# A block of dilated attention and gated delta rule: ScalarE's functions grouped by table, z's columns behind the keys', the decays' sums beside the values, levels of the inverse by a counted wait

## The chip, the core and the metric

The kernel runs on one core of a Trainium2 chip. The core has TensorE (matmuls, in the profile PE, its weight loads PEld), VectorE (DVE), ScalarE (ACT), GpSimd (POOL) and SyncE (SP), which issues nearly all DMAs here. Each engine works through its own queue in order, and engines wait for each other by semaphores. The metric is device time in microseconds, the median of some runs. The profile is of one execution; its TensorE clock is given as the share of full speed that was granted.

## What is computed

One transformer block over 1024 tokens of width 1024, in float32: modulation by a vector c, an RMS norm, one projection of 3600 columns, attention over dilated windows (8 heads of 64), a gated delta rule (8 heads of 64), an output projection, and a gated feed-forward part. The change lies in the delta rule:

```python
def _gated_deltanet(q, k, v, z, b_logit, a_logit, conv_w, a_log, dt_bias, norm_g):
    qkv = silu(_causal_conv(concatenate([q, k, v], -1), conv_w))     # four taps
    q, k, v = split(qkv, 3, -1)                                      # 8 heads of 64
    q = _l2norm(q) * HEAD_DIM ** -0.5
    k = _l2norm(k)
    beta = sigmoid(b_logit)
    g = -exp(a_log) * softplus(a_logit + dt_bias)
    o = _chunk_gated_delta_rule(q, k, v, g, beta)
    return _rmsnorm(o, norm_g) * silu(z)
```

Within a chunk the sums of g over the tokens (gcum) give decays exp(gcum_i - gcum_j); the keys' products with each other, times decay and beta, are a strictly lower triangular matrix A; I + A is inverted against the values and keys; then the state goes from chunk to chunk:

```python
    v_new = u_i - w_i @ state
    o_i = (q_i * exp(g_i)) @ state + qk_i @ v_new
    state = state * exp(g_last) + (k_i * exp(g_last - g_i)).T @ v_new
```

The modulation is `silu(c) @ w_ada + b_ada`, six vectors of 1024; the later ones are needed only after attention.

## The kernel before

**Tiling.** Activations are kept transposed, 128 of the 1024 features to a partition tile and 1024 tokens along the free axis. A product at float32's precision is three matmuls: weights and activations are split into a rounded part (hh, wh) and a rest (hl, wl), with the pairs hh-wh, hl-wh, hh-wl. `wsplit` (L209) loads a slab of weights through SyncE, ScalarE rounds it (L215), GpSimd takes the rest (L216); there are 3 raw and 5 split buffers. The kernel works on chunks of 128 tokens, eight of them, for two groups g of four heads.

**Filler.** Projections that nothing waits for yet come from a generator, `others` (L1103), a unit at a time: a unit of `proj_d` (L571) is three matmuls of 512 columns and is counted as 0.64 us, one of `proj_t` (L579) three of 256 columns, counted as 0.32. These counts are nominal. Its order is z of group 0 (20.48 us nominal), then keys kd, queries qd and values vd of group 1 (20.48 each), z of group 1, the attention's values (40.96), and its keys and queries (81.92). `mixed` (L1123) adds one row of the modulation (`modulation`, L1081: a DMA of 256 KB, four small matmuls, L196) whenever 1.9 us of filler have gone by, unless `quiet` is set; there are 64 rows in 8 sums, all in one PSUM bank, and after each sum VectorE turns it (L203) and adds the bias (L207).

**Order.** A scheduler puts the instructions on the queues at build time: it takes, for each engine, what it reckons to be ready, in the program's order, unless something is marked urgent. `tc.issue_after(i)` only fixes issue order: what is traced inside comes behind i on i's engine. Where delta-rule work would come too early on TensorE, `turn(name)` (L552) looks up FILL (L41): so much filler is traced first, and the step is issued behind its last matmul. `hold` (L1136) does the same ahead of the levels of the inverse: it traces filler until a named projection is done (`until`, L1143) and then so many us more (LEVELS, L31: group 0 "qd" and 4, group 1 "z1" and 28). These are lower bounds: the scheduler can still put later filler in front.

**The front.** The projections of the first keys and queries (their second half L600 to L605) and of values end at about 113 us. `decays` (L645 to L668) makes, in three PSUM banks, the sums Gc of the decays within a chunk (L654, L655), their totals (L657, and ScalarE's Exp L658), edec and eG (L660, L661), and Gc transposed (L663), which goes to DRAM as G and comes back as rows for each head (`delta_rows`, L680), masked on GpSimd (L692).

**A group of the delta rule** (`delta`, L1163). Conv and Silu of keys and queries (`conv`, L529; Silu at L536); transposes and squares (`delta_turn`, L705); Ln (L1175 in group 0, L741 in group 1) and Exp (L743) of the keys' sums of squares, the root; 32 Exps of the decay tiles dt (L747); the products of keys with keys and queries (L776, the kk products) and VectorE's products with the decays (L782); stores of the diagonal 32x32 blocks (L789); Exp of the rows for the queries (L815); conv, Silu, transposes (L833) of the values (`delta_v`); then `delta_inverse` (L843): the blocks come back as nt, VectorE inverts all of them in 31 dependent double steps (L862, L866), stores them (L869) and reads them back as tn (L871). The levels put the 128x128 inverses together from them for four heads (L894 lv, L909, L913, L923 lw, L931 lx). `delta_scan` (L945) then goes through the chunks. Between the groups `delta_early` (L1152) does the conv, Silu and squares of group 1's keys and queries. z's columns go through Silu on ScalarE as each block leaves PSUM (`z_evac`, L611). After group 1 come attention with the rest of the filler, the output projection and the feed-forward part, which the change does not touch.

## Time and profile before

| what | us |
|---|---|
| median of 3 runs | 1498.29 (1481.16 to 1502.68) |
| the profiled execution | 1498.45 |
| its span | 1496.7 |
| TensorE busy | 1405.0 |
| VectorE, ScalarE, GpSimd busy | 873.6, 669.6, 302.2 |
| granted clock, mean | 0.961 |

The stages that matter, by their first and last instruction on TensorE: front to 113.5 us, group 0 up to the levels 113.5 to 241.1, its levels to 267.2, its scan, the early part of group 1 and group 1 up to its levels to 412.8, these levels to 449.5, group 1's scan to 491.7, then filler alone to 522.3, and attention. A busy TensorE at a granted clock of 0.5 does half the work; idle time of an engine that bounds nothing costs nothing. In a row of the profile the last bracket holds the idle time of the engine before the instruction and what ended it.

### The profile page before, as it was taken

Reading aid. Unit: us, or ns where it says so; the run is one execution under the profiler, and the core shown is the slowest. Engines: PE = TensorE matmul, PEld = TensorE weight load, DVE = VectorE, ACT = ScalarE, POOL = GpSimd, SP = SyncE. Lnnn points to the kernel's source line nnn. Section 1 sums busy time; section 2 is a strip of 40 time slices with the busy share of each in tenths; the row PEclk is TensorE's granted clock in tenths of the full one; section 3 lists DMA queues with packets and bytes.
Section 4 is the critical chain, followed back from the end, with each engine's and each line's share of the span. In section 5 each row is a group of like instructions: output and inputs, shape, how many; then the busy total and the mean of one; then the engine's idle time right before and its main releaser. Section 6 shows DMA issues by size and latency. Waiting matters only on the chain. (4 is left out here: it accounts for less than half of the span.)

```text
span 1496.7 us, 24578 instructions
## 1 busy us (share of the span) xinstructions
PE 1405.0 (94%) x8984; PEld 1140.2 (76%) x8984; DVE 873.6 (58%) x1664; ACT 669.6 (45%) x1283; POOL 302.2 (20%) x275
## 2 busy tenths in 40 slices
PE   7998989988999989999998899999999999999986
PEld 4677857867888768777876678888888888878765
DVE  3786843665736041466327986757575755454675
ACT  3487413357123353676337633333333333445453
POOL 2344412335104332444253000000000000000011
PEclk9998999999959999999999999999999999999998
DMA  8736563475502526633384374535363636656664
GB/s 307 249 94 170 142 205 122 146 241 142 165 20 78 167 84 166 186 106 109 104 263 141 108 245 136 197 121 199 116 205 106 216 107 202 226 191 191 192 206 164
DMA packets 171345, 244.64 MB, mean 163 GB/s; under 512 B 33014, under 2 KB 76327, under 8 KB 171224
## 3 DMA queue, kind: packets, MB, share of 16 engines
q1 hardware_dynamic: 171224, 243.07, 52.0%
q8 instruction: 71, 1.16, 0.4%
q14 instruction: 50, 0.41, 0.1%
HBM read 180.25 MB, written 67.48 MB: 166 GB/s over the span
## 5 line engine op out<-in xcount | busy, mean ns | idle before, releaser
L1747 POOL TENSOR_TENSOR y<-y,gfr 128x512 f32<-128x512 f32 x8 | 12.9, 1633 | 669.4 <-DMA xr<-x_d 639.6
L1502 DVE TENSOR_TENSOR wl_db<-wr_db,wh_db 128x512 fp32r<-128x512 f32 x77 | 54.2, 704 | 95.1 <-ACT wh_db L1501 95.1
L1501 ACT CAST wh_db<-wr_db 128x512 fp32r<-128x512 f32 x77 | 48.0, 623 | 112.7 <-PE X L1690 58.6
L1690 PE MATMUL X<-wl_db,wh_da 128*128 128x512 f32 x176 | 71.4, 406 | 9.1 <-DVE wl_db L1502 9.1
L1690 PE MATMUL X<-wh_db,wl_da 128*128 128x512 f32 x176 | 70.9, 403 | 0.0
L1690 PE MATMUL X<-wh_db,wh_da 128*128 128x512 f32 x176 | 68.3, 393 | 0.0
L1263 POOL TENSOR_SCALAR X<-X,sc 128x128 f32<-128x128 f32 (+7 forms) x64 | 48.0, 753 | 69.5 <-DVE sc L1262 55.9
L1261 ACT ACTIVATE X<-X,sc 128x128 f32<-128x128 f32 (+7 forms) x64 | 49.5, 775 | 22.3 <-DVE sc L1256 16.6
L1256 DVE CUSTOM_DVE_ANT_0 X<-S,ng 128x512 f32<-128x512 f32 (+3 forms) x64 | 36.9, 586 | 33.5 <-PE S L1253 22.5
L1502 DVE TENSOR_TENSOR wl_da<-wr_da,wh_da 128x512 fp32r<-128x512 f32 x77 | 53.9, 700 | 3.6 <-ACT wh_da L1501 3.6
L567 PE MATMUL wo<-yh,wh_wo 128*128 128x512 f32 x128 | 53.1, 416 | 2.4 <-ACT yh L1359 1.7
L1222 DVE SCALAR_TENSOR_TENSOR QS<-raw,QS 64x1024 fp32r<-64x1024 f32 x8 | 12.6, 1573 | 70.5 <-ACT QS L1221 70.5
L567 PE MATMUL wo<-yh,wl_wo 128*128 128x512 f32 x128 | 51.4, 403 | 0.0
L567 PE MATMUL wo<-yl,wh_wo 128*128 128x512 f32 x128 | 51.1, 401 | 0.0
L1501 ACT CAST wh_da<-wr_da 128x512 fp32r<-128x512 f32 x77 | 47.4, 615 | 7.5 <-PE wua L1512 5.8
L567 PE MATMUL g_a<-hh,wh_a 128*128 128x512 f32 x128 | 50.6, 395 | 0.0
L567 PE MATMUL g_a<-hh,wl_a 128*128 128x512 f32 x128 | 50.5, 395 | 0.0
L567 PE MATMUL g_a<-hl,wh_a 128*128 128x512 f32 x128 | 50.3, 393 | 0.0
L1293 PE MATMUL y<-et,va 128*64 128x128 f32 x576 | 47.7, 288 | 1.3 <-ACT et L1281 1.3
L1690 PEld LDWEIGHTS X<-wl_db,wh_da 128*128 128x128 f32 x176 | 34.4, 195 | 18.3 <-DVE wl_db L1502 11.0
L1501 ACT CAST wh_wg_s<-wg_s 128x512 fp32r<-128x512 f32 x33 | 20.4, 622 | 57.4 <-PE wga L1512 19.1
L1276 PE MATMUL tr<-ident,X 128*128 128x128 f32 x288 | 44.2, 279 | 1.3 <-ACT et L1281 1.2
(530 smaller groups left out, 4456.0 us busy)
## 6 DMA issues: line engine op xcount, KB each, us to landing
wr_da<-ao_d SPq DMA_DIRECT2D x77, 256.0 KB, 3.0
wm<-in_wada SPq DMA_DIRECT2D x64, 256.0 KB, 3.9
wr_wg<-in_wg SPq DMA_DIRECT2D x48, 256.0 KB, 3.1
wr_wu<-in_wu SPq DMA_DIRECT2D x48, 256.0 KB, 2.7
wr_wd<-in_wdn SPq DMA_DIRECT2D x44, 256.0 KB, 3.2
ao_d<-a SPq DMA_DIRECT2D x44, 256.0 KB, 3.0
wr_db<-wt_d SPq DMA_DIRECT2D x44, 256.0 KB, 2.6
ao_d<-as SPq DMA_DIRECT2D x33, 256.0 KB, 2.0
```

The costliest lines, as they stand in the source:

```text
L567: last[0] = nc.tensor.matmul(ps, a[:, w0], b[k0 + k4][:, cs], start=(i == 0), stop=(i == n - 1))
L1222: nc.vector.scalar_tensor_tensor(out=QS[low], in0=raws[0][low], scalar=-0.125, in1=QS[low].bitcast(F32), op0=ALU.mult, op1=ALU.subtract,)
L1256: nc.vector.tensor_tensor_reduce(out=X[:, c0:c1], in0=ps[:, 0 : c1 - c0], in1=ng[:, u + c0 : u + c1], scale=1.0, scalar=(3e38 if m is None ...
L1261: nc.scalar.activation(X[:, 0:nk], X[:, 0:nk], AF.Exp, scale=-1.0, bias=m, accum_out=sc[:, 2:3])
L1263: nc.gpsimd.tensor_scalar(out=X[:, 0:nk], in0=X[:, 0:nk], scalar1=sc[:, 3:4], scalar2=0.0, op0=ALU.mult, op1=ALU.add)
L1276: nc.tensor.transpose(ps[:, (kb - c0) * P : (kb - c0 + 1) * P], X[:, kb * P : kb * P + P], ident)
L1293: nc.tensor.matmul(yps[64 * e : 64 * e + 64, yc], va[:, kb, 64 * e : 64 * e + 64], ets[e][:, kb, :], start=(kb == 0), stop=(kb == qb),)
L1501: nc.scalar.copy(hi, src)
L1502: (eng or nc.vector).tensor_tensor(out=lo, in0=src, in1=hi.bitcast(F32), op=ALU.subtract)
L1690: nc.tensor.matmul(bank[b], a[:, ts_], w, start=(first and f == 0 and n_ == 0), stop=(f == NF - 1 and n_ == 2), skip_group_check=True,)
L1747: nc.gpsimd.tensor_tensor(out=t, in0=t, in1=gfr[:, dsl[s]], op=ALU.mult)
```

## The change

It does five things.

1. ScalarE's functions are grouped. `conv` notes its Silus; the Ln of the keys' squares is issued behind the last of them, in both groups in `delta_prep`; the three Exps of the decays (edec, eG, eGl) follow group 0's root, and the Exps of the queries' rows are issued behind the root.
2. The filler's order becomes kd, z of group 0, qd, vd, z of group 1, with the rest as before.
3. The decays are no longer a function behind the second half of the queries' projection but stand before it, marked urgent, so that they fall into the values' matmuls. They use one PSUM bank (`abank`) for the three results, and VectorE instead of ScalarE takes the totals out.
4. The levels' wait is counted: `spent` adds up all filler traced; `st["kk"]` notes it after the kk products; the levels come 44 us of it later in group 0, 48 in group 1. The waits for projections at the scan change to z, and qd is asked for before `delta_early`. FILL gets eleven entries for group steps of the front (5.76 us nominal up to group 0's kk products).
5. `quiet` is set from the start until group 0's kk products have been traced, and the modulation's first row is issued behind the last of them. Its bank is cleared once at the start and then a quarter at a time, behind each of the first four sums.

```diff
-LEVELS = ("qd", 4), ("z1", 28)
+LEVELS = 44.0, 48.0
 FILL = {
+    "trq1_0False": 1.92,
+    "bp0": 1.28,
+    "kk0_0_1_k": 0.64,
+    "kk0_2_0_k": 0.64,
+    "kk0_2_1_k": 0.64,
+    "trq2_0False": 1.92,
+    "trq3_0False": 2.56,
+    "bp1": 2.56,
+    "kk1_0_1_k": 0.64,
+    "kk1_2_0_k": 0.64,
+    "kk1_2_1_k": 0.64,
...
-        nc.scalar.activation(dst, dst, AF.Silu)
+        silus.append(nc.scalar.activation(dst, dst, AF.Silu).ins)
...
             us -= w
+            spent[0] += w
...
+    dbank = abank("decays")
+    with urgent():
+        nc.tensor.matmul(dbank[:, 0:64], tri, t2, start=True, stop=True)
+        nc.vector.tensor_scalar(out=Gc, in0=dbank[:, 0:64], scalar1=-1.0, scalar2=None, op0=ALU.mult)
+        nc.tensor.matmul(dbank[:, 64:128], ones, t2, start=True, stop=True)
+        nc.vector.scalar_tensor_tensor(
+            out=edec, in0=dbank[:, 64:128], scalar=-1.0, in1=Gc, op0=ALU.mult, op1=ALU.subtract
+        )
+        nc.vector.tensor_scalar(out=eGl, in0=dbank[:, 64:128], scalar1=-1.0, scalar2=None, op0=ALU.mult)
+        nc.tensor.transpose(dbank[:64, 128 : 128 + P], Gc, ident)
+        GT = pd.tile([64, P], F32, name="GT", tag="nbpT", bufs=1)
+        nc.vector.tensor_copy(GT, dbank[:64, 128 : 128 + P])
         nc.sync.dma_start(_.G, GT)
...
-        if g == 1:
+        with tc.issue_after(silus[-1]):
             nc.scalar.activation(lr, rk, AF.Ln, bias=eps1)
         nc.vector.tensor_scalar(out=lr, in0=lr, scalar1=-0.5, scalar2=None, op0=ALU.mult)
-        nc.scalar.activation(rk, lr, AF.Exp)
+        root = nc.scalar.activation(rk, lr, AF.Exp)
         nc.vector.tensor_tensor(out=lr, in0=lr, in1=g3(Gc), op=ALU.subtract)
+        if g == 0:
+            for e, x in ((edec, edec), (eG, Gc), (eGl, eGl)):
+                nc.scalar.activation(e, x, AF.Exp)
...
+        with turn(f"bp{g}"):
+            nc.tensor.transpose(ps[:32, 0:P], nbp.rearrange("p n h -> p (n h)"), ident)
...
+        st["kk"] = spent[0]
+        quiet[0] = False
...
-            nc.scalar.activation(eb, eb, AF.Exp)
+            with tc.issue_after(root.ins):
+                nc.scalar.activation(eb, eb, AF.Exp)
...
-            with hold(*LEVELS[g]) if step == 0 else ExitStack():
+            with hold(st["kk"] + LEVELS[g] - spent[0]) if step == 0 else ExitStack():
...
         pm = ybank("mods")
+        nc.vector.memset(pm, 0.0)
...
-            if i % 4 == 0:
-                nc.vector.memset(pm, 0.0)
...
-                rows4(ps, cc[:, k : k + 32], w, 4, k == KT - 1)
+                with tc.issue_after(kk_last[0].ins) if (i, k) == (0, 0) else ExitStack():
+                    rows4(ps, cc[:, k : k + 32], w, 4, k == KT - 1)
...
+            if i < 4:
+                nc.vector.memset(ps, 0.0)
...
+        yield from group1(("kd",))
         yield from proj_t(I["wz0"], 256, "z0", z_evac(0))
-        yield from group1(("kd", "qd", "vd"))
+        done.add("z0")
+        yield from group1(("qd", "vd"))
         yield from proj_t(I["wz1"], 256, "z1", z_evac(1))
...
-    quiet = [False]
+    quiet = [True]
...
-    def hold(what, us):
-        until(lambda: what in done)
-        while us > 0:
-            us -= next(fill[0])
+    def hold(us):
+        ahead(us)
         return tc.issue_after(last[0].ins)
...
-                if j == 1:
-                    nc.scalar.activation(norms[0]["lr"], norms[0]["rk"], AF.Ln, bias=eps1)
...
-        until(lambda: ("qd", "z1")[g] in done)
+        until(lambda: ("z0", "z1")[g] in done)
         delta_scan(g, st)
         if g == 0:
+            until(lambda: "qd" in done)
             delta_early()
```

More of the change, by code (lines that the diff above doesn't have):

```diff
@@ L597, in run @@
             pass
-    for q in range(2):
-        ps = gbank(f"g_qd{q}")
-        cs = slice(HALF, T)
-        run(gemm(ps, [(wsplit(I["wd"][8 + q, s], HALF, f"qd{q}_{s}"), 4 * s) for s in range(2)], hh, hl, cs))
-        with urgent():
-            nc.scalar.copy(xps[2 + q][:, cs], ps)
     def z_evac(g):
@@ L644, in build @@
     nc.scalar.activation(t2, t2, AF.Exp, scale=-1.0)
[L645 to L663 removed]
+    nc.scalar.activation(t2, t2, AF.Ln, bias=ones[:, 0:1])
@@ L664, in decays @@
         GT = pd.tile([64, P], F32, name="GT", tag="nbpT", bufs=1)
-        nc.vector.tensor_copy(GT, ps[:64, 0:P])
+        nc.vector.tensor_copy(GT, dbank[:64, 128 : 128 + P])
         nc.sync.dma_start(_.G, GT)
-    decays()
+    for q in range(2):
+        ps = gbank(f"g_qd{q}")
+        cs = slice(HALF, T)
+        run(gemm(ps, [(wsplit(I["wd"][8 + q, s], HALF, f"qd{q}_{s}"), 4 * s) for s in range(2)], hh, hl, cs))
+        with urgent():
+            nc.scalar.copy(xps[2 + q][:, cs], ps)
     S = [[const([P, P], f"S{q}_{i}") for i in range(3)] for q in range(2)]
```

31 lines of the change are left out of this document (10 added, 21 removed).

## The prediction

> **What bounds the kernel now.** I read the page first, then the windows of its stages, then the waits of TensorE, then ScalarE's groups, then single rows of the time line around the waits.
>
> ```profile
> PE 1405.0 (94%) x8984; PEld 1140.2 (76%) x8984; DVE 873.6 (58%) x1664; ACT 669.6 (45%) x1283; POOL 302.2 (20%) x275
> ...
> PEclk9998999999959999999999999999999999999998
> ```
>
> TensorE is busy for 1405 of 1496.7 us and no other engine for more than 58%, so the span is TensorE's work, plus the time it idles, plus what it loses while its granted clock is low. The change can only win in the last two. The clock row shows one deep hole, the 5 in the twelfth slice (412 to 449 us). The windows of the stages tell where both lie; columns are the stretch, its length, then busy us (and instructions) of PE, PEld, DVE, ACT and POOL, the granted clock, the DMA share and GB/s. Stretches run from the end of the first projections (113.5) to group 0's levels of the inverse (241.1 to 267.2), to group 1's levels (412.8 to 449.5), to the end of group 1's scan.
>
> ```profile
> 113.50:241.10 127.60, 116.79 (x853) 89.77 (x851) 74.53 (x129) 56.96 (x111) 43.86 (x35) 0.92 0.63 177
> 241.10:267.20 26.10, 25.88 (x503) 19.15 (x502) 15.12 (x27) 10.49 (x24) 5.68 (x6) 1.00 0.28 86
> 267.20:412.80 145.60, 131.24 (x1149) 114.36 (x1148) 90.79 (x208) 64.68 (x133) 51.98 (x48) 0.96 0.59 173
> 412.80:449.50 36.70, 36.70 (x513) 33.09 (x514) 13.14 (x28) 10.20 (x26) 3.18 (x4) 0.58 0.04 13
> 449.50:491.70 42.20, 38.46 (x299) 35.16 (x296) 25.95 (x88) 13.11 (x38) 18.47 (x20) 1.00 0.27 76
> 491.70:522.30 30.60, 30.60 (x137) 25.34 (x138) 1.22 (x1) 9.25 (x20) 8.39 (x7) 1.00 0.66 189
> ```
>
> Idle: 127.6 - 116.8 = 10.8 us before group 0's levels, 0.2 in them, 145.6 - 131.2 = 14.4 up to group 1's. The same levels take 26.1 us at clock 1.00 and 36.7 at 0.58: 10.6 us lost. The last row is projection filler alone: 30.6 us for 137 matmuls, 0.223 us each. Filler that is not used early lands in such a dense stretch and costs the same there, so moving it is free in itself. The stretches of half clock, with the same columns:
>
> ```profile
> 136.46:150.11 13.65, 12.37 (x84) 11.58 (x86) 7.76 (x17) 10.40 (x27) 5.20 (x4) 0.50 0.45 126
> 191.07:197.90 6.83, 6.21 (x27) 4.03 (x28) 6.35 (x19) 0.00 (x0) 0.00 (x0) 0.50 0.35 116
> 331.02:337.85 6.83, 5.30 (x25) 5.30 (x26) 5.33 (x9) 5.80 (x11) 0.73 (x1) 0.50 0.75 259
> 354.91:358.33 3.41, 3.41 (x22) 2.81 (x21) 0.58 (x1) 3.38 (x4) 1.81 (x1) 0.50 0.43 125
> 412.94:443.66 30.72, 30.72 (x409) 27.76 (x405) 12.03 (x27) 8.12 (x21) 3.18 (x4) 0.50 0.03 11
> ```
>
> Work at half clock takes twice as long, so half of the busy time is lost: (12.37 + 6.21)/2 = 9.3 us before group 0's levels, (5.30 + 3.41)/2 = 4.4 up to group 1's. What TensorE waited for (total, times, longest):
>
> ```profile
> PE mods L196 <- DMA wm<-in_wada: 4.6, 3, 2.8
> PE mods L196 <- DVE mt L203: 4.3, 2, 3.9
> PE lv L894 <- DMA tn<-tn_d: 3.4, 1, 3.4
> PE trq_0False L714 <- ACT cv L536: 3.3, 1, 3.3
> PE kk_k L776 <- DVE qk L782: 3.0, 2, 2.6
> PE ps_GT L663 <- DVE Gc L655: 2.0, 1, 2.0
> PE ps_bp L757 <- DVE nbp L751: 1.8, 1, 1.8
> ```
>
> Each half-clock stretch begins at the end of one of these waits (2.6 to 3.9 us long). All that can be won: 10.8 + 9.3, then 14.6 + 4.4, then 10.6, in sum 49.7 us, 3.3% of the span.
>
> **The change, part by part.**
>
> *Functions by table.* ScalarE reloads its table 18 times from 88 to 500 us, 1.283 us each:
>
> ```profile
> L536 ACT ACT_TABLE_LOAD x6 | 7.7, 1283 | 0.1
> ...
> L611 ACT ACT_TABLE_LOAD x3 | 3.8, 1283 | 0.1
> L747 ACT ACT_TABLE_LOAD x3 | 3.8, 1283 | 0.1
> ...
> L743 ACT ACT_TABLE_LOAD x2 | 2.6, 1283 | 0.0
> ...
> L658 ACT ACT_TABLE_LOAD x1 | 1.3, 1283 | 0.0
> L1175 ACT ACT_TABLE_LOAD x1 | 1.3, 1283 | 0.0
> L741 ACT ACT_TABLE_LOAD x1 | 1.3, 1283 | 0.0
> L815 ACT ACT_TABLE_LOAD x1 | 1.3, 1283 | 0.0
> ```
>
> With Ln behind the last query's Silu, the decays' three Exps behind the root and z's Silus pushed later, each group needs Ln, Exp, Silu once: 7 loads, 11 fewer, 14.1 us of ScalarE. Between 113.5 and group 0's inverse there are 8 now and 3 then (6.4 us less), before group 1's 9 and 3 (7.7 less). None is TensorE time by itself: they shorten the chain Exp, kk products, inverse, tn. Against it stands that Ln now waits for the last Silu and its load, 1.6 us with the Ln itself (I put it at 0.3). The Trainium skill, page ScalarE: Activation LUTs, section What ACT_TABLE_LOAD costs, gives a 1283 ns load plus a drain of about 1380 ns for each switch. The load agrees to the nanosecond; the drain does not show in this trace, where the idle column is 0.1 us for six loads. By the page the chain would shorten by 6.9 us more in group 0, an estimate, and the sum would come out some 3 us lower, at 1472.
>
> *Counted waits.* Levels used to follow 61.4 + 4 us of filler (nominal) in group 0 and 102.4 + 28 in group 1; now 44 and 48 after the keys' products, by when 5.8 and 71.0 are counted: 49.8 and 119.0. The inverse's side, from rows of VectorE, SyncE's read of tn, TensorE and ScalarE:
>
> ```profile
> 200.23 0.19 DVE L866 TENSOR_TENSOR tt<-tt,tm 128x31 f32<-128x31 f32 x1
> ```
> ```profile
> 412.84 0.43 DVE L899 STREAM_TRANSPOSE U<-tn 32x256 f32<-32x256 f32 x1 [7.84 <-DMA tn<-tn_d]
> ```
> ```profile
> 139.48 0.60 ACT L720 ACTIVATE sqq<-trq_0False 128x512 f32<-128x512 f32 x1 [3.56 <-PE trq_0False L714]
> ```
>
> Group 1's VectorE waited 7.84 us from its last inverse step to tn's landing. Group 0's steps ended at 200.4, so tn stood ready at 208.2 and its levels began at 241.1: 33 us of cover, which the change spends. In the new order tn comes earlier by the loads (6.4), by the 3.56 us that ScalarE waited for a transpose queued behind a modulation row whose weights were late (those rows now start after the kk products), less 1.6 to 2.6 for Ln: at 198 to 201. TensorE's work up to the levels needs three prices:
>
> ```profile
> L833 PE MATMUL trv<-ident,vd 128*128 128x128 f32 x16 | 2.1, 276 | 1.1 <-ACT vd L536 1.1
> ```
> ```profile
> 340.00:354.40 14.40, 10.45 (x128) 8.92 (x128) 1.00 0.52 120
> ```
> ```profile
> 200.03:202.66 2.63, 2.34 (x10) 1.62 (x10) 1.00 0.35 75
> ```
>
> A transpose is 2.1/16 = 0.13 us; a group's 128 kk matmuls are 10.45; nine filler matmuls and one modulation row are 2.63, so a row is 2.63 - 9 x 0.223 = 0.62. Then 49.8 nominal (keys 20.5, z 20.5, queries 8.8) is about 53 us (a unit of 0.64 is three matmuls, 0.67; z's I take 8% over nominal), 44/1.92 = 23 rows are 14.3, kk 10.5, 48 transposes 6.3: 84 us, and from 113.5 TensorE would stand at the levels at 197.5. The same sum for before gives 108 of work, plus 10.8 and 9.3, against 127.6 on the clock, so it closes within 1 us. Idle is then at least 0.5 to 3.5 us; the modulation's sums still wait for VectorE inside the inverse (4.3 before), part of it in the same idle. I take 6 idle and 2 at half clock, between 1 and 20: gain 20.1 - 8 = 12. What hides the inverse is filler alone; where that runs out each late us is a us of span, and the levels then start cold.
>
> From group 0's levels to group 1's: 171.7 us before, of which 14.6 idle and 4.4 lost to the clock, so 152.7 of work. Now 69.2 nominal instead of 64.5 (5 us) and some 6 rows more (3.7): 161.4. The chain is 171.7 - 7.7 = 164, so 2.6 idle at least. The waits for the query's Silu, the betas' transpose and the kk products (8.1 in the table above) get fillers of 2.56, 2.56 and 0.64 in front. I take 6 idle, 1 clock: gain 19.0 - 7 = 12.
>
> *Decays in one bank, inside the values' matmuls.* The 2.0 us wait for Gc leaves its place; three handovers between VectorE and TensorE in one bank come at about 91 us instead, each between 0 and that 2.0 us: I take 1 for all, up to 6. SyncE's store of G and the four row loads and POOL's selects behind them come some 20 us sooner, off the chain.
>
> *z behind the keys.* Same matmuls, same DMAs; the order changes on SyncE and in POOL's and ScalarE's splits. Total filler is unchanged, so nothing by itself. Group 1's values stay at 81.9 nominal in the order while their chain comes some 40 us sooner; their last matmul starts at 308.63, their second convolution at 362.09, so that slack covers it:
>
> ```profile
> 308.63 0.40 PE L567 MATMUL g_vd<-hh,wl_vd 128*128 128x512 f32 x1
> ```
> ```profile
> 362.09 1.15 ACT L530 ACTIVATE vd<-xp_v,cw 128x1024 f32<-128x1024 f32 x1 [1.89 <-PE trv L833]
> ```
>
> The values come later against the chain by the 16 us of filler (65.4 - 49.8) that the levels no longer wait for; of the 53 us some 37 are left. Without that cover each us would be idle before lv. Modulation's memsets: one of 512 columns out, four of 128 in, on VectorE under the filler; a row that starts behind one waits with it, which is in the 6.
>
> Sum: -12 - 12 + 1 = -23, with one of the two groups' levels still at half clock as now. The profiled execution is 1498.45 us (span 1496.7), as good as the median 1498.29 (runs 1481.16 to 1502.68): 1475.
>
> **The rivals.**
> *Both levels warm* (1464): if the last wait before lv stays under about 2.6 us in both groups, the 10.6 us go too. For: the two sums above miss by 0.5 to 3.5 us only. Against: a 2.6 us wait (kk) was enough to halve the clock.
> *Both cold* (1486): tn late by over 2.6 us twice; 10.6 more. For: before, lv waited 3.4 us and the cover in group 0 is gone.
> *Clock returns early* (1468): one group starts cold but gets the clock back after 6.8 us, as at 331, and loses 3.4 instead of 10.6. Against: the only levels that started cold stayed so for 30.7 us with TensorE busy throughout. The Trainium skill, page TensorE: Matmul & The Clock Gate, Part 1, has the clock back after one busy window of some 3.4 us; by that rule this case would be the likely one, and the row at 412.94 disagrees.
> *The chain is not shortened* (1495): convolutions on VectorE, not loads, set it. Then tn lands at 208 and 10.7 + 10.3 us of idle and cold levels in both groups give back nearly all.
> *Slower* (1505): Ln held behind the last Silu lengthens the chain. Each us late at lv is now a us of span in each group, where group 0 had 33 to spare. From 23 - 10.6 = 12.4 us late over both groups, levels cold, it is slower than before; at 20 us, 1505.
>
> **How the numbers follow.** Forecast 0.38, both warm 0.27, clock early 0.10, both cold 0.13, chain not shortened 0.07, slower 0.05. The likeliest is 1475, its own range 1466 to 1484. From 1450 (both warm, 14 us of idle less than I take) to 1496 leaves out the last case and the tails. Two per cent, about what a measurement of this kernel can tell from no change, is 1468.3 and 1528.3: faster 0.27 + half of the 0.10 + 0.08 of the forecast's lower tail = 0.40; slower 0.03; within 0.57.
>
> **What would show it.** Right: about 7 loads, none between a group's 32 Exps; no modulation row before the kk products; lv of group 0 near 200, of group 1 near 365; idle before lv under 4 us; the stretch before group 0's levels near 92 us instead of 127.6. Wrong: tn late by over 5 us, more than one group's levels at 0.5, waits for DVE mt above 5 us, or a z Silu amid the Exps.

## The result, and the profile after

The changed kernel runs in 1468.19 us (median of 4 runs, 1467.06 to 1475.44), the kernel before in 1490.03 us (median of 4, 1481.16 to 1502.68): ratio 0.989 [0.984, 0.994]. Forecast were 1475 us and a range of 1450 to 1496. A second series gave 1466.9 us (6 runs, 1462.68 to 1470.72), ratio 0.987 [0.981, 0.992]; 79 runs of the kernel before, taken beside the experiments below, lie between 1475.1 and 1508.6. The ratios leave out executions more than 1.5% above the fastest of their kernel, the medians and spreads here don't. The profiled execution of the changed kernel took 1467.1 us (span 1465.4), that of the kernel before 1498.45.

The top of the page of the changed kernel:

```profile
PE 1382.0 (94%) x8984; PEld 1119.5 (76%) x8984; DVE 874.5 (60%) x1668; ACT 655.9 (45%) x1273; POOL 298.8 (20%) x275
...
PEclk9999999999999999999999999999999999999998
```

The 5 in the clock row is gone. TensorE has 23 us less busy time for the same 8984 matmuls: less of that work runs at half clock. The windows of the stages, with the columns of the prediction (stretch, length, then busy us and instructions of PE, PEld, DVE, ACT and POOL, granted clock, DMA share, GB/s). The stretches run from 88 to the end of the first projections (now 120.3), to group 0's levels, through these, to group 1's levels, through these, to attention; the last three rows are the stretches at half clock:

```profile
88.00:120.30 32.30, 27.64 (x234) 21.90 (x233) 25.40 (x30) 23.68 (x36) 20.06 (x13) 0.89 0.51 134
120.30:214.37 94.07, 87.38 (x699) 69.25 (x697) 67.25 (x117) 42.57 (x89) 30.42 (x28) 1.00 0.53 150
214.37:242.90 28.53, 27.31 (x509) 20.20 (x508) 18.78 (x36) 13.68 (x31) 5.74 (x6) 1.00 0.37 114
242.90:392.70 149.80, 140.97 (x1192) 117.33 (x1191) 92.75 (x210) 58.31 (x132) 55.55 (x49) 0.98 0.62 183
392.70:417.90 25.20, 25.20 (x532) 21.99 (x533) 13.12 (x28) 10.58 (x27) 5.79 (x7) 1.00 0.36 100
417.90:498.50 80.60, 79.04 (x521) 70.60 (x522) 26.65 (x91) 24.35 (x62) 27.06 (x27) 1.00 0.41 118
109.16:115.99 6.83, 6.04 (x14) 4.83 (x15) 3.80 (x3) 2.22 (x5) 6.83 (x5) 0.50 0.46 115
303.72:307.14 3.42, 3.42 (x18) 2.25 (x17) 1.24 (x3) 3.39 (x6) 0.00 (x0) 0.50 0.73 242
354.92:358.34 3.42, 3.42 (x22) 2.70 (x20) 2.68 (x11) 0.00 (x0) 0.95 (x1) 0.50 0.06 8
```

and of the kernel before, the stretch that the prediction left out:

```profile
88.00:113.50 25.50, 24.61 (x236) 20.36 (x236) 21.94 (x25) 21.48 (x32) 16.22 (x10) 1.00 0.22 63
```

Read them so. Both groups' levels now run at clock 1.00 (group 1's take 25.2 us; they took 36.7). Only three half-clock stretches are left between 88 and 498 us, 13.7 us together, where there were 61.4. But the first of them, 109 to 116, is new, and the first projections end at 120.3 instead of 113.5. What TensorE waited for between 88 and 500 us (total, times, longest):

```profile
PE trv L854 <- ACT vd L548: 4.2, 2, 2.9
PE g_qd L583 <- POOL hl L470: 4.2, 1, 4.2
PE trq_0False L728 <- ACT cv L548: 3.3, 2, 2.4
PE mods L208 <- DVE mods L1118: 1.6, 1, 1.6
...
PE mods L208 <- DVE mt L215: 1.3, 1, 1.3
...
PE lv L915 <- DMA tn<-tn_d: 0.4, 1, 0.4
```

The modulation's waits for its weights (4.6 us) are gone, those for mt fell from 4.3 to 1.3, a memset costs 1.6; lv's fell from 3.4 to 0.4; and 4.2 us for hl are new (0.9 before). ScalarE's table loads from 88 to 498 us:

```profile
L548 ACT ACT_TABLE_LOAD x2 | 2.6, 1283 | 0.0
L755 ACT ACT_TABLE_LOAD x2 | 2.6, 1283 | 0.0
L757 ACT ACT_TABLE_LOAD x2 | 2.6, 1283 | 0.0
L761 ACT ACT_TABLE_LOAD x1 | 1.3, 1283 | 0.0
L619 ACT ACT_TABLE_LOAD x1 | 1.3, 1283 | 0.0
```

Eight instead of 18: Ln and Exp once for each group, Silu three times (L548 twice, then with z's at L619), and one for the decays' Exps (L761).

To compare kernels I use the *front*: from the first product of the values to attention's first product, 3726 to 3728 matmuls in every kernel here. One window over it, for the kernel before and the changed one:

```profile
75.30:522.20 446.90, 416.87 (x3728) 347.01 (x3726) 252.18 (x520) 196.27 (x400) 148.96 (x130) 0.93 0.49 141
```
```profile
75.90:498.50 422.60, 399.63 (x3726) 330.93 (x3725) 252.99 (x524) 183.04 (x390) 145.98 (x130) 0.98 0.51 149
```

446.9 to 422.6 us: 24.3 less, of which idle time makes 7.1 (446.9 - 416.9 = 30.0, now 23.0) and busy time, that is the clock, 17.2. The remaining 7 of the 31.3 us between the two spans lie outside the front, nearly all behind it (974.5 us, now 966.9), where the change does nothing.

One reservation holds for all that follows. Both profiled executions of the kernel before are long ones, with a mean clock of 0.961 here and 0.953 in r9. Of its 79 runs the 32 with 0.970 or more took 1475 to 1486 us (median 1479.3), the 30 with 0.961 or less 1492 to 1509. All ten runs of the change had 0.972 or more. So the 24.3 us stand against a long execution, and where the half clock of a shorter one lies no profile shows.

### The profile page after: what moved, and what is told of

It reads as the page before. It is cut to its first block, busy times and chain, and to the rows that moved or that the text cites. A ratio compares the mean times of both kernels' runs of the same rounds, so it can differ in the third digit from the quotient of the medians.

```text
span 1465.4 us, 24581 instructions
## 1 busy us (share of the span) xinstructions
PE 1382.0 (94%) x8984; PEld 1119.5 (76%) x8984; DVE 874.5 (60%) x1668; ACT 655.9 (45%) x1273; POOL 298.8 (20%) x275
## 4 chain that ended last, share of the span: by engine, by line
PE 44%; issue 15%; DVE 4%; DMA 3%; POOL 1%; ACT 1%; POOLq 0%; SPq 0%; DVEq 0%; ACTq 0%
PE wua L1534 8%; PE wga L1534 7%; PE g_a L583 5%; PE wuc L1534 4%; PE wo L583 4%; PE wgc L1534 4%; PE y L1315 2%; PE tr L1298 2%; PE wub L1534 2%; PE wgb L1534 1%; PE S L1274 1%; PE X L1712 1%; PE S L1275 1%; DMA xp_d<-xo 1%; DVE x L1493 0%
## 5 line engine op out<-in xcount | busy, mean ns | idle before, releaser
L1244 DVE SCALAR_TENSOR_TENSOR QS<-raw,QS 64x1024 fp32r<-64x1024 f32 x8 | 12.6, 1570 | 81.2 <-ACT QS L1243 81.2
L1283 ACT ACTIVATE X<-X,sc 128x128 f32<-128x128 f32 (+7 forms) x64 | 49.5, 775 | 22.8 <-DVE sc L1278 17.2
```

Source lines behind the costliest of these rows:

```text
L1283: nc.scalar.activation(X[:, 0:nk], X[:, 0:nk], AF.Exp, scale=-1.0, bias=m, accum_out=sc[:, 2:3])
```

## The experiments

All twelve runs; r9 and r10 are the two kernels themselves again. "Idle" is the front less TensorE's busy time in it. lv is when the levels begin, counted from the start of the front.

| kernel | ratio to before | front, idle, clock | lv group 0, group 1 |
|---|---|---|---|
| before (first profile) | 1 | 446.9, 30.0, 0.93 | 165.9, 337.5 |
| r9 before again | - | 454.6, 28.5, 0.91 | 163.7, 338.7 |
| the change | 0.989 [0.984, 0.994] | 422.6, 23.0, 0.98 | 138.5, 316.8 |
| r10 the change again | 0.987 [0.981, 0.992] | 423.0, 22.9, 0.98 | 138.6, 317.2 |
| e1 selects behind hl | 0.986 [0.979, 0.992] | 421.1, 23.9, 0.99 | 136.5, 315.3 |
| r12 e1 and one filler entry | 0.989 [0.986, 0.993] | 419.5, 24.8, 0.99 | 136.7, 313.0 |
| e2 rows behind nt's read | 1.002 [0.998, 1.005] | 435.3, 38.1, 0.97 | 136.3, 326.1 |
| e3 old waits | 0.993 [0.989, 0.997] | 426.7, 31.1, 0.99 | 162.5, 330.2 |
| e4 before, counted waits alone | 0.994 [0.990, 0.998] | 436.1, 24.4, 0.94 | 141.3, 326.6 |
| e5 z first | 0.992 [0.987, 0.998] | 441.3, 26.5, 0.94 | 139.5, 332.6 |
| e6 functions as before | 1.001 [0.997, 1.006] | 451.7, 36.9, 0.93 | 150.6, 329.7 |
| r11 before, functions alone | 1.004 [1.000, 1.009] | 445.2, 25.9, 0.93 | 164.3, 336.5 |
| e7 rows from the start | 0.995 [0.990, 0.999] | 430.8, 34.0, 0.98 | 136.4, 323.8 |
| e9 28 us ahead of group 1 | 0.994 [0.988, 0.999] | 428.7, 28.4, 0.97 | 138.9, 319.3 |

The idle time repeats in the two pairs of profiles that there are (30.0 and 28.5, 23.0 and 22.9); the clock does not always (446.9 and 454.6 us for the same order of work). So I read a difference in idle above 2 us from one profile, but not one in the clock.

**e1_selects_behind.** The changed kernel, with this:

```diff
-            nc.gpsimd.tensor_tensor(out=hl[k][:, cs], in0=xt[:, cs], in1=hh[k][:, cs].bitcast(F32), op=ALU.subtract)
+            rests.append(nc.gpsimd.tensor_tensor(
+                out=hl[k][:, cs], in0=xt[:, cs], in1=hh[k][:, cs].bitcast(F32), op=ALU.subtract
+            ).ins)
...
-            sel[g] = nc.gpsimd.affine_select(
+            with tc.issue_after(rests[-1]):
+                sel[g] = nc.gpsimd.affine_select(
```

It tests what the new wait for hl costs. GpSimd's time line in the changed kernel (start, us, engine, line, operation, idle before):

```profile
102.43 1.46 POOL L706 TENSOR_SCALAR_AFFINE_SELECT dt<-dt 128x1024 f32<-128x1024 f32 x1
103.86 1.30 POOL L228 TENSOR_TENSOR wl_qd<-wr_qd,wh_qd 128x512 fp32r<-128x512 f32 x1
105.11 1.29 POOL L228 TENSOR_TENSOR wl_kd<-wr_kd,wh_kd 128x512 fp32r<-128x512 f32 x1
107.58 1.09 POOL L706 TENSOR_SCALAR_AFFINE_SELECT dt<-dt 128x1024 f32<-128x1024 f32 x1 [1.17 <-DMA dt<-G_d]
108.63 1.26 POOL L470 TENSOR_TENSOR hl<-xt,hh 128x512 fp32r<-128x512 f32 x1
```

Two selects of the decay tiles stand ahead of hl, the second one waiting for its DMA; before, hl ran at 103.2.

> The changed kernel, with GpSimd's four selects of group 0's decay tiles held behind its last split of the tokens (hl). My theory: the 4.2 us that TensorE waits at 109.95 for hl come from the select that stands in front of it in GpSimd's queue (102.4 to 108.6, it waits for a DMA), and the half clock from 109.2 to 116.0 comes from that wait. Then the wait falls under 1.5 us, the clock stays up there, the second half of the queries' projection ends near 113 instead of 120.3, and the time falls by 5 to 8 us against the changed kernel's 1468 (ratio to before about 0.980 to 0.986). Rival: hl is late for another reason (ScalarE's three Exps and two table loads at 93 to 100 us), then hl starts at about 105 at best, TensorE still waits over 2.5 us, the clock still halves, and the time stays within 2 us of 1468. Second rival: the 7 us are won there, but the levels follow tn, so that they begin at 214 as now and the 7 us stand as idle or early filler: 1465 to 1468.

Measured: the wait fell from 4.2 to 1.3 us and the half clock at 109 to 116 went. The selects were the cause. But the front is only 1.5 us shorter, the idle time no less (23.9), ratio 0.986 [0.979, 0.992]. TensorE's next wait in e1, and ScalarE's in front of it:

```profile
121.04 1.11 PE L733 MATMUL trk_1False<-ident,kd 128*128 128x128 f32 x4 [2.85 <-ACT kt L741]
```
```profile
119.91 0.60 ACT L739 ACTIVATE sqk<-trk_1False 128x512 f32<-128x512 f32 x1 [3.02 <-DVE rk L743]
```

The transposes wait for ScalarE's copy, which waits for VectorE, which is busy with the convolutions. Of the 5 to 8 us that I expected, 2 arrive at group 0's levels; the rest moved to the next member of the same chain, much as in the second rival.

**e2_rows_after_read.** The changed kernel, with `quiet` lifted only when nt has been asked for, and the first modulation load issued behind that read:

```diff
         st["kk"] = spent[0]
-        quiet[0] = False
...
-        nc.sync.dma_start(nt.rearrange("p j i -> p (j i)"), _.lt[g])
+        nt_read[0] = nc.sync.dma_start(nt.rearrange("p j i -> p (j i)"), _.lt[g])
+        quiet[0] = False
...
-                with urgent():
+                with tc.issue_after(nt_read[0].ins) if (i, k) == (0, 0) else ExitStack(), urgent():
                     nc.sync.dma_start(w, I["wada"][k * P : (k + 1) * P, t0 * P : t0 * P + HALF])
```

In the changed kernel SyncE's queue between the kk products and the inverse reads (start, us):

```profile
155.43 0.37 SPq L807 DMA_DIRECT2D lt_d<-dt  x1
157.44 0.33 SPq L1111 DMA_DIRECT2D wm<-in_wada  x1
157.82 0.42 SPq L807 DMA_DIRECT2D lt_d<-dt  x1
...
165.06 0.35 SPq L1111 DMA_DIRECT2D wm<-in_wada  x1
165.45 0.43 SPq L807 DMA_DIRECT2D lt_d<-dt  x1
...
169.24 0.33 SPq L867 DMA_DIRECT2D nt<-lt_d  x1
```

Each load of a modulation row (wm) waits for one of three buffers, which TensorE frees when it has done a row, and the stores of the blocks stand behind it: 10.5 us for eight stores that took 5.2 in one go in the kernel before.

> The changed kernel, with the first modulation row's load issued behind the read of nt on SyncE (quiet until then). My theory: the read of nt at 169.2 is late because eight of the sixteen stores ahead of it stand between modulation loads that wait for a buffer; then nt is read near 160, VectorE's inverse starts near 166 instead of 176, and tn is there near 204. TensorE had no gap at 214.4, so the ten us were covered by filler: the levels may begin up to 10 us earlier, the filler runs later, and the time moves by less than 3 us (1465 to 1471). Rival: the lateness of tn is a us of span for each us, as my prediction had it: 1458 to 1460. Second rival: the missing modulation rows leave holes at 152 to 165 (waits for the values), where the clock drops: 1470 to 1476.

Measured: nt is read at 159.0, and VectorE's inverse starts 10 us earlier, counted from the start of the front. Group 0's levels begin only 2 us earlier: the lateness had been covered by filler, as I said. But by the ratio (1.002) the whole gain is lost, and none of my theories had the place: 164 us between the levels instead of 150, 25.9 of them idle. TensorE's two largest waits there:

```profile
PE mods L208 <- DMA wm<-in_wada: 7.8, 7, 2.0
PE g_z L607 <- ACT sp_vd L1089: 4.3, 1, 4.3
```

The second of them, seen from ScalarE, in e2 and then in e7 (below), where the same wait is 5.3 us long:

```profile
341.45 0.89 ACT L1089 COPY sp_vd<-g_vd 128x256 f32<-128x256 f32 x2 [13.33 <-DMA pj_d<-sp_vd]
```
```profile
335.97 0.73 ACT L1088 COPY sp_vd<-g_vd 128x256 f32<-128x256 f32 x2 [11.97 <-DMA pj_d<-sp_vd]
```

ScalarE takes the filler's results to sp_vd, and it waits for the stores that make sp_vd free. On SyncE these stores stand behind loads that wait for buffers (in e7 modulation loads at 324.3, a load of weights and modulation loads again at 330.2, then two stores of blocks, then these at 332.8). So TensorE stops because nothing takes its results away; e6 has the same with other tiles. This is read from the traces; no run took the stores out of that queue.

**e3_old_waits.** The changed kernel with the old waits:

```diff
-LEVELS = 44.0, 48.0
+LEVELS = ("qd", 4), ("z1", 28)
...
-            with hold(st["kk"] + LEVELS[g] - spent[0]) if step == 0 else ExitStack():
+            with hold(*LEVELS[g]) if step == 0 else ExitStack():
...
-    def hold(us):
+    def hold(what, us):
+        until(lambda: what in done)
```

> The changed kernel with the levels' old waits (queries' filler and 4 us in group 0, z of group 1 and 28 us in group 1) instead of the counted 44 and 48. My theory: the counted waits bring the levels forward only where the chain is ready; with the old ones group 0's levels begin some 12 to 16 us later (226 to 231), group 1's some 10 to 15 us later, the filler for that is taken from the stretch behind group 1's scan, no idle is added, and both levels stay warm: within 4 us of 1468. Rival: the old waits are what made group 1's levels cold and the idle in front: then the stretch before group 1's levels has 5 us more idle, its levels take 36 instead of 26 us, and the time goes back to 1480 or more.

Measured: levels later by 24 and 13 us, both at clock 1.00 as my theory had it, but 8 us more idle in front of them, as the rival had it (31.1). Front 4.1 us longer, ratio 0.993 [0.989, 0.997].

**e4_counted_only.** The kernel before with

```diff
-LEVELS = ("qd", 4), ("z1", 28)
+LEVELS = 49.8, 119.0
...
+            spent[0] += w
...
-            with hold(*LEVELS[g]) if step == 0 else ExitStack():
+            with hold(LEVELS[g] - spent[0]) if step == 0 else ExitStack():
...
```

> The kernel before with the counted waits alone (49.8 and 119.0 nominal us of filler ahead of the levels, all that was traced from the start counted; z's columns stay ahead of the keys'). My theory: group 0's tn is ready at 208, the filler before the levels runs out some 16 us nominal earlier, so the levels begin near 215 to 222 and stay warm; in group 1 the chain is as late as before, the filler ahead is gone, and lv waits for tn by 3 us or more, so the levels run at half clock as before: 1482 to 1492, within 1% of before (ratio 0.995 to 1.003). Rival: the counted wait by itself carries most of the 22 us: 1468 to 1474 (ratio under 0.990).

Measured: idle falls from 30.0 to 24.4, nearly to that of the whole change, and the levels of group 0 come 25 us sooner. The clock stays at 0.94: the half-clock stretches before the kk products and at 189 us are there as before, and group 1's levels take 31.9 us. Against my theory lv did not wait for tn there; 13.7 us of these levels ran at half clock all the same. Ratio 0.994 [0.990, 0.998], about half of the change's gain.

**e5_z_first.** The changed kernel with the old order of the filler:

```diff
-        yield from group1(("kd",))
         yield from proj_t(I["wz0"], 256, "z0", z_evac(0))
         done.add("z0")
-        yield from group1(("qd", "vd"))
+        yield from group1(("kd", "qd", "vd"))
```

> The changed kernel with the filler's old order, z of group 0 ahead of the keys of group 1. My theory: the order costs nothing by itself except that z's Silus then fall among group 0's Exps (137 to 150 us) and bring 2 to 4 table loads back, and the keys of group 1 come later, behind group 0's levels at most by 20 us, which their slack covers: 1468 to 1473. Rival: the order is what lets the levels start without a gap; with it undone the stretch up to group 0's levels idles 5 us more and the clock drops: 1475 to 1482.

Measured: loads rise from 10 to 15 in the front, as expected; idle is 26.5, most of the other 15 us is group 0's levels at half clock for 34.1 us. I don't put that down to the order: the largest wait ahead of them in these levels was 1.2 us, as in the changed kernel (0.7 to 1.2), where the clock held. Ratio 0.992 [0.987, 0.998]: the times don't settle whether the order is worth anything.

**e6_tables_old.** The changed kernel with ScalarE's functions as before (group 0's Ln stands in `delta` again, behind the second key):

```diff
         nc.sync.dma_start(_.G, GT)
+    for e, x in ((eGl, eGl), (edec, edec), (eG, Gc)):
+        nc.scalar.activation(e, x, AF.Exp)
...
-        with tc.issue_after(silus[-1]):
+        if g == 1:
             nc.scalar.activation(lr, rk, AF.Ln, bias=eps1)
...
-        if g == 0:
-            for e, x in ((edec, edec), (eG, Gc), (eGl, eGl)):
-                nc.scalar.activation(e, x, AF.Exp)
...
-            with tc.issue_after(root.ins):
-                nc.scalar.activation(eb, eb, AF.Exp)
+            nc.scalar.activation(eb, eb, AF.Exp)
```

> The changed kernel with ScalarE's functions in the old order (Ln of the keys' squares as soon as they are there, the decays' three Exps beside their sums, nothing held behind the root). My theory: table loads between 88 and 500 us rise from 10 to 14 or more, the root comes later by 3 to 6 us in each group, the kk products wait for it, and the clock drops once more before them: 4 to 10 us slower than 1468 (1472 to 1478). Rival: the loads are off TensorE's path, as they were before: within 2 us of 1468 although the loads are back.

Measured: 17 loads instead of 10 in the whole front, idle 36.9, front 29 us longer, ratio 1.001 [0.997, 1.006]: without this part nothing is left of the gain. Of the 29 us, 12 lie ahead of group 0's levels, 1 between the levels and 16 from group 1's levels on, where 30.7 us (423.5 to 454.2) ran at half clock. The 12 are in part what I expected: the root comes 4.2 us later, counted from the start of the front, the last kk product 9.5, and four half-clock stretches (17.1 us together) stand between 126 and 206, where the change has none. But TensorE hardly idles at the kk products. Its longest waits (the second is 5.3 us), and what ScalarE and SyncE did in front of the longest:

```profile
PE g_z L606 <- ACT zt L619: 12.6, 2, 7.4
```
```profile
352.17 1.15 ACT L542 ACTIVATE vd<-xp_v,cw 128x1024 f32<-128x1024 f32 x1 [8.23 <-DMA xp_v<-pj_d]
358.33 0.74 ACT L619 ACTIVATE zt<-g_z 128x256 f32<-128x256 f32 x2 [5.01 <-DMA zg_d<-zt]
```
```profile
350.77 1.28 SPq L1109 DMA_DIRECT2D wm<-in_wada  x3
352.11 0.42 SPq L1170 DMA_DIRECT2D xp_v<-pj_d  x1
352.62 0.85 SPq L625 DMA_DIRECT2D zg_d<-zt  x2
```

It is the filler that waits. z's Silu on ScalarE needs one of two zt buffers; these come free when their stores land. GpSimd had finished both at 344.8, but their stores were issued at 352.6: they stand on SyncE behind reads of xp_v and modulation loads, which wait for TensorE's rows. And TensorE cannot go on with z while nothing takes its results away. e5 has the same at 363 us (7.6 us). That chain is read from the trace; no run gave zt a third buffer.

**r11_tables_only.** The kernel before with the functions grouped and nothing else, so the same places the other way round:

```diff
-        if g == 1:
+        with tc.issue_after(silus[-1]):
             nc.scalar.activation(lr, rk, AF.Ln, bias=eps1)
...
+        if g == 0:
+            for e, x in ((edec, edec), (eG, Gc), (eGl, eGl)):
+                nc.scalar.activation(e, x, AF.Exp)
...
```

> The kernel before with ScalarE's functions grouped alone: Ln behind the last query's Silu in both groups, the decays' three Exps behind group 0's root (VectorE takes the totals out), the queries' row Exps behind the root; waits, filler order, modulation and decays' place as before. Undoing this part in the changed kernel cost 29 us of the front. My theory: by itself it is worth much less, since group 0's levels have 33 us of cover there and wait for the queries' filler: fewer table loads (20 to 14 to 16, z's Silus still fall among the Exps), group 0's levels begin within 4 us of before, group 1's chain is 5 to 8 us shorter, lv waits less: 2 to 10 us faster than before (ratio 0.993 to 0.999). Rival: it is the carrier of the gain alone: ratio under 0.990. Second rival: Ln behind the last Silu makes it later, and the kk products wait: ratio over 1.000.

Measured: 14 loads instead of 20 in the whole front; group 0's first kk product starts 57.6 us into the front instead of 65.2. But the 7.6 us don't reach the end of the chain: the last kk product starts at 78.6 instead of 81.2, nt is read at 88.9 instead of 86.3, tn at 129.0 instead of 130.8. And the levels, which the old wait keeps behind the queries' filler, begin at 164.3 instead of 165.9, group 1's at 336.5 instead of 337.5. Ratio 1.004 [1.000, 1.009]: by itself the part wins nothing.

**e7_rows_free.** The changed kernel with the modulation's rows let go from the start:

```diff
-                with tc.issue_after(kk_last[0].ins) if (i, k) == (0, 0) else ExitStack():
-                    rows4(ps, cc[:, k : k + 32], w, 4, k == KT - 1)
+                rows4(ps, cc[:, k : k + 32], w, 4, k == KT - 1)
...
-    quiet = [True]
+    quiet = [False]
```

> The changed kernel with the modulation's rows allowed from the start, not held behind group 0's kk products. My theory: rows whose weights are late stand again among the transposes and kk products of 120 to 150 us, as they did before (waits of TensorE for wm 2.8 us and of ScalarE 3.6 us), the half clock at 136 to 150 comes back, and the time rises by 5 to 9 us: 1473 to 1477. In exchange SyncE's stores of the blocks are no longer between the loads of rows, and nt is read some us earlier. Rival: the rows fill the gaps that are there now at 120 to 174 (6 us of idle), and nothing is lost: 1464 to 1469.

Measured: slower, but again in another place. No half clock comes back at 136 to 150, and the stretch up to group 0's levels has 11.7 us idle (11.4 in the changed kernel). nt is read 86.3 us into the front, 7 us sooner than in the changed kernel, as I expected; the levels begin 2 us sooner. Between the levels 21.6 us are idle instead of 8.8, the longest on waits for wm (5.1) and for ScalarE's outlet of the filler (5.3), like e2's. Ratio 0.995 [0.990, 0.999].

**e9_levels_28.** The changed kernel with less filler ahead of group 1's levels:

```diff
-LEVELS = 44.0, 48.0
+LEVELS = 44.0, 28.0
```

> The changed kernel with 28 instead of 48 nominal us of filler ahead of group 1's levels. My theory: VectorE's inverse and tn set their start (tn lands at 392.7 now, just as the filler ends); with 20 us less filler TensorE idles before lv by up to 15 us unless the scheduler puts other filler there by itself, the clock is at half when the levels begin and stays there: the levels take 36 instead of 26 us, and the time rises by 12 to 25 us, to 1480 to 1493. Rival: the scheduler fills by its own reckoning of when tn is ready, and the number hardly matters: within 3 us of 1468, levels at full clock.

Group 1's lv on TensorE's time line, then the windows of its levels and of the half-clock stretch around their start:

```profile
393.88 1.33 PE L915 MATMUL lv<-tn,dt 32*32 32x32 f32 x42 [6.96 <-DMA tn<-tn_d]
```
```profile
393.90:421.30 27.40, 27.40 (x532) 24.07 (x532) 13.14 (x28) 10.84 (x27) 4.45 (x5) 0.90 0.30 92
389.26:399.50 10.24, 5.62 (x116) 5.33 (x119) 3.44 (x8) 3.31 (x8) 1.27 (x1) 0.50 0.77 186
```

Without the filler TensorE waits 7.0 us for tn, and the front has 5.4 us more idle; the levels begin no sooner (319.3), since tn sets their start. But the clock came back after 10.2 us, in the middle of the levels, and they took 27.4 us, not 36.

**r9_before_again, r10_after_again.** The two kernels once more.

> The kernel before, once more, for a second profile of it. My theory: its times (56 of them beside the runs so far, 1475 to 1509) differ by which of its gaps fall so that the clock goes to half: the edges of all half-clock stretches lie on one grid of 3.41 us, and the grid lies differently against the work in each execution. Then the order and TensorE's idle time are as in the first profile (front of 447 us from the first product of the values to attention: idle 30 us within 1.5), and the lost half-clock time differs from its 30.6 us there, so that the front is 425 to 447 us. If group 1's levels again take 37 us at half clock, with lv behind a wait for tn over 3 us, cold levels belong to the wait, as my prediction had it. Rival: levels at full clock although lv waits over 3 us; then the wait does not decide it.

> The changed kernel once more, with more runs. My theory: both levels at full clock, front of 421 to 424 us, and the runs bunch at 1465 to 1470 with few above 1475, since only short half-clock stretches are left: median 1467 to 1471, ratio to before 0.984 to 0.992. Rival: that both levels were at full clock was luck of one execution; then a third or more of the runs lie at 1478 to 1490 (one hole of 30 us at half clock costs 10 to 17 us), and the median is 1472 or more.

The kernel before again has group 1's levels cold, now for 51 us; lv had waited 3.75 us for tn:

```profile
412.68:463.88 51.20, 50.72 (x561) 46.58 (x562) 15.48 (x39) 12.07 (x31) 4.80 (x6) 0.50 0.04 12
```

and that execution took 1500.78 us. The changed kernel again has both warm (lv does not wait at all), and its six runs lie between 1462.7 and 1470.7 us.

**r12_no_key_wait.** e1 with one entry more in FILL:

```diff
+    "trk1_0False": 1.92,
     "bp0": 1.28,
```

> The changed kernel with the selects behind hl, as in e1_selects_behind, and 1.92 nominal us of filler ahead of the transposes of the second key's first half, where e1_selects_behind waited 2.85 us for ScalarE at 121.0 and lost the clock to 123.9. My theory: that wait goes under 1 us, the half clock there goes, 3 us of idle and 1.4 of clock are won in the stretch up to group 0's levels; the filler is only moved: front 417 to 420 us, median 1461 to 1465. Rival: the idle shows up at the next wait in the chain (the betas' transpose, the values'), since ScalarE and VectorE set the pace there: within 2 us of e1_selects_behind, 1464 to 1468. Second rival: as with the other small moves (e2, e7) the modulation's rows and z's columns of group 1 fall otherwise, and the stretch between the levels idles 10 us more: 1474 to 1482.

Measured: the wait at 121 us is still 2.84 us. My entry was one step off: it puts filler ahead of the second key's first half, and the transposes that wait are its second half. So this run says nothing of that wait. Its time, 0.989 [0.986, 0.993], can't be told from that of the change. Its 12 runs lie between 1462.0 and 1492.6 us.

## Why the prediction was right, and where it was not

*The bound* held: TensorE's work is unchanged, and all that was won is idle time and half clock. The sum was -23 us; in the profiled executions the front won 24.3. Its split was not as I put it.

| term | forecast | measured |
|---|---|---|
| up to group 0's levels | -12 + 1 (idle 10.8 to 6, clock 9.3 to 2, decays +1) | -6.6 (from 88 us: idle 11.7 to 11.4, clock 9.3 to 3.0) |
| between the levels | -12 (idle 14.6 to 6, clock 4.4 to 1) | -5.6 (idle 14.6 to 10.0, clock 4.4 to 3.4) |
| group 1's levels | 0 (one group still cold) | -11.5 (36.7 to 25.2) |

So the case that I gave 0.27, both levels warm (1464), is the one that came. And what is left of idle and half clock in the first two rows, which I put at 15 us, is 27.8. The two errors, some 11 us each, cancelled: that the sum came out was luck. And the third row is seen only against a long execution of the kernel before (clock 0.961); whether its shorter ones have cold levels no profile shows. Against their median of 1479.3 us the ten runs of the change (median 1467.5) win some 12 us; the idle time makes 5.5 to 7.1 of them if it is the same in shorter executions, which is not shown.

*Decays in one bank.* I priced three handovers at 1 us; TensorE waited 0.5 us at 91. But of the selects on GpSimd I wrote that they come sooner "off the chain". That step failed: they went past hl in GpSimd's queue, and TensorE waited 4.2 us and lost 3.0 more to half clock. e1 shows the cause, and that taking it away wins next to nothing, since VectorE's convolutions come next.

*Levels of group 0 at 197.5.* They began at 214.4. The difference: 6.8 us for the later end of the first projections, 3.4 us more work than I reckoned (87.4 against 84) and 6.7 idle, 16.9 in sum. (Group 1's began at 392.7 instead of near 365: these 17 us, 6.4 more of idle and half clock between the levels, and some 4 more of work.)

tn was late as well: the inverse ended at 206.7, and I had put tn at 198 to 201, earlier by the table loads and by ScalarE's wait of 3.56 us. That step failed. SyncE's reads of nt (before) and of tn (before, then changed; nt's read at 169.24 is shown under e2):

```profile
161.60 0.32 SPq L846 DMA_DIRECT2D nt<-lt_d  x1
206.13 0.38 SPq L871 DMA_DIRECT2D tn<-tn_d  x1
```
```profile
209.94 0.37 SPq L892 DMA_DIRECT2D tn<-tn_d  x1
```

The same from the start of each front (us), with the start of group 0's last kk product and of its levels:

| kernel | last kk | nt read | tn read | levels |
|---|---|---|---|---|
| before | 81.2 | 86.3 | 130.8 | 165.9 |
| r11, functions alone | 78.6 | 88.9 | 129.0 | 164.3 |
| e4, counted waits alone | 79.7 | 84.7 | 129.7 | 141.3 |
| the change | 74.9 | 93.3 | 134.0 | 138.5 |
| e2, rows behind nt's read | 73.9 | 84.3 | 121.4 | 136.3 |
| e7, rows from the start | 72.0 | 86.3 | 127.7 | 136.4 |
| e6, functions as before | 84.4 | 106.7 | 146.2 | 150.6 |

The changed kernel does its kk products 6 us sooner, but reads nt 7 us and tn 3 us later than the kernel before. The modulation rows that moved behind the kk products put their loads in front of nt's read on SyncE; e2 and e7 take them away and have nt 7 to 9 us sooner. I had counted the rows on TensorE and not their loads on that queue. It cost 2 us of the levels' start, since counted filler covered the rest. So what brings group 0's levels forward by 27 us is the cover that the counted wait spends, and not a shorter chain.

*Functions by table.* 8 loads between 88 and 500 us against 7: the decays' Exps are behind the root in the program, but not held there, and the scheduler took them at 94.3 with a load of their own. r11 has the first kk product 7.6 us sooner, as large as I put it (6.4 plus 3.56 less 1.6 to 2.6), but tn only 1.8, and alone the part is worth nothing; e6 shows that the change without it is worth nothing either. The table reconciles the two: with the other four parts and the old functions tn is read at 146.2, 16 us later than in e4, where the old functions stand beside the counted waits alone. So in the changed kernel the grouping keeps the chain from getting longer than the counted filler can cover. Which of the other parts would lengthen it no run shows.

*Counted waits.* e4 and e3 bear out that they take the idle time (4.1 to 5.6 us alone, 8.1 where undone) and spend the cover. In both profiles of the change lv waits 0.4 us or nothing, as the filler just lasts until tn lands.

*Cold levels.* My rule was that a wait above 2.6 us at lv makes them cold for good. For it: waits of 3.43, 3.75 and (r11, just ahead of lv) 2.59 us were followed by 30.7, 51.2 and 30.7 us at half clock, and 0.4 and 0 by none. Against it: e9 (7.0 us, clock back after 10.2), e5, whose levels went cold behind 1.2 us, e4 (13.7 us at half clock in group 1's, behind 1.0 us) and e6 (30.7 us that began 19 us into group 1's levels, behind no wait above 0.5 us). Of the 28 levels in the 14 profiles, the four behind a wait of 2.59 us or more all ran at half clock in part or whole, and of the other 24 these three. So the wait goes with the half clock more often than not, and does not decide. What does decide is open. The page TensorE: Matmul & The Clock Gate of the Trainium skill, Part 1, lets the clock return after one busy window of some 3.4 us; the stretches of 30.7 to 51.2 us inside levels, with TensorE busy throughout (50.72 of 51.20), do not agree, as far as the profile's busy time is what the page means by busy.

*The rest of the span*, which the change does not touch, made 7 us between the two profiled executions. The forecast stood against an execution of 1498.45 us, one of the longer ones beside the 79; against the median of 1490.03, which four runs gave, the same 23 us give 1467, and 1468.19 was measured.

Open: what z's order and the rows' hold are worth, and the decays' place and the entries in FILL, which no run undid alone. Undone one at a time, the parts lengthened the front by 29.1 (e6), 18.7 (e5), 8.2 (e7) and 4.1 us (e3), 60 in sum, where all together won 24. They are not terms of a sum, and the clock's share in each, large in e5 and e6, is one execution's.

## What to carry to other kernels

An instruction moved earlier passes others on each queue that it uses: list who stands behind it on GpSimd and SyncE too, above all behind loads that wait for a buffer. When an edit shortens a chain, read the time at the chain's last member: of 7.6 us at the first kk product 1.8 were left at tn (r11), and where a fixed wait stands behind the chain, nothing is won. Test each part alone and each undone, since the two answers can differ (r11 and e6). Where a kernel's runs spread by 2%, compare TensorE's idle time in a fixed stretch of the work: in the two pairs here it repeats within 1.5 us where the time does not.

## What the hardware showed that I had not expected

Half-clock stretches begin and end on a grid of 3.413 us: in the changed kernel the starts at 109.16 and 303.72 are 57 steps apart, and all their lengths in the fronts of all 14 profiles (3.41, 6.83, 10.24, 13.65, 30.72, 34.13, 51.20 us) are whole numbers of steps. The grid lies differently against the work in each execution. So the same wait can cost a stretch of half clock or none, and the same order of work gave fronts of 446.9 and 454.6 us. Nor does a stretch begin just at the end of a wait, as I read it in the prediction: in the kernel before one began at 331.02, 1.5 us ahead of the end of a wait, and one at 354.91, 1.8 us behind.
